# A two-layer mLSTM and retention trunk: order of the state product, one score split on VectorE, later rotary tables, and a last row tile in two column groups

## The chip, the cores and the metric

The kernel runs on one core of one Trainium2 chip. The metric is the device time of one execution in microseconds (us); the median of several runs is compared. The profile records one execution with its own time.

## The reference

Two layers of a pre-norm trunk on 1024 tokens of width 1024. Each layer makes one combined projection, feeds four mLSTM heads and four retention heads of 256, gates and normalises each head, multiplies with the output matrix, and adds the result to x. A last RMSNorm follows.

```python
for l in range(DEPTH):
    shift, scale, gate = jnp.split(c_act @ w_ada[l] + b_ada[l], 3, axis=-1)
    h = rmsnorm(x, norm_g[l]) * (1.0 + scale[:, None, :]) + shift[:, None, :]
    mq, mk, mv, mo, mz, mi, mf, rq, rk, rv, rz = split_cols(h @ w_in[l])
    qk = jax.nn.silu(causal_dwconv(jnp.concatenate([mq, mk], axis=-1), conv_w[l], conv_b[l]))
    ...
    y_m = jax.nn.sigmoid(mo) * head_layernorm(cell, gn_m[l], N_HEADS_MLSTM) * jax.nn.silu(mz)
    rq_h = rotary(rq.reshape(B, S, N_HEADS_RET, HD_R), positions)
    rk_h = rotary(rk.reshape(B, S, N_HEADS_RET, HD_R), positions)
    ...
    y_r = head_layernorm(ret, gn_r[l], N_HEADS_RET) * jax.nn.silu(rz)
    y = jnp.concatenate([y_m, y_r], axis=-1) @ w_out[l]
    x = x + gate[:, None, :] * y
return rmsnorm(x, final_g)
```

`rotary` turns the two halves of q and k by angles position x frequency, for the retention heads alone.

## The kernel before, in words

**Products in three matmuls.** Every operand of a product is held as a high part in a short float format and a low part, the rest of it. `mm3` issues high x high, high x low and low x high into one PSUM bank. `split_to(dst, src, eng)` makes the two parts: ScalarE copies (L614), and `eng` subtracts (L615); GpSimd is the default, and the state's split names VectorE.

**Order.** TensorE's order is written by hand. A unit is a piece of TensorE work with what empties its bank; `run_units` calls `tick()` after each. `launch(gen, delay)` puts a generator of side work on a list, and `tick` runs those that are due; the number that a generator yields is the count of steps until its next piece. What comes of this as an order of calls decides TensorE's instructions. The other engines' orders follow from these calls through a scheduler that places each instruction on its engine; once built, every engine runs strictly in its order, and waits at an instruction whose data or buffer isn't ready.

**A layer.** Per head group hg (0 to 3 mLSTM, 4 to 7 retention): `gate_path` (z and o columns), `qk_ml` or `qk_ret` (q, then k), and `v_path`. They write four PSUM banks `pp` in turn. For mLSTM, `conv_silu` reads a bank with VectorE products (L632), takes three columns over from the half before (L634), goes through a tanh on ScalarE (L636) and a product (L637). For k the result is also transposed (L644) and stored to DRAM; `k_rows` reads it back. `v_split` reads a bank with ScalarE (L600) and VectorE (L601).

**Attention** runs as side work beside the projections of the next group, on four banks `pa`. Four pieces of 256 tokens, j = 0 to 3; those in `WHOLE` are taken as one, the others as two tiles of 128. `scores(j)` multiplies q and k, applies the mask `dm` (from a transfer, L748 and L750, and an exponential) with VectorE (L780 or L789, then L790), and splits the result into `sH` and `sL`. `update` adds to the running state `cf` (L818) and splits it into `cH` and `cL` on VectorE. `values(j, tts)` multiplies q with the state parts (j > 0; L839 takes it to `nd`), then the scores with v, and L851 adds the two.

**Rotary tables.** `rotary_tables` makes, in four pieces of 256 positions, the reduced angles for sine and cosine. Each piece is one load of positions (L374), 26 VectorE instructions on three 512-wide tiles taken from the pool `g` (six tiles, shared with the gates of L543 and L553), and two stores to the DRAM tensors `rdr` (L403). `a1`, half of one of those tiles, is written by a copy early in each piece (L378) and is the source of the cosine's store. `load_rotary` reads `rdr` back when head group 3's attention ends. The launch stands at the end of head group 1's turn in layer 0.

**The end.** `out_units` multiplies with the output matrix. For the last half and column block (`done` given) twelve of the sixteen k pieces go over four row tiles together, into four banks; the last four go row tile by row tile. After each, `out_evac` multiplies by the gate (L997), adds x (L998), and sums squares (L1001). `final_rows` then makes the row's scale with a power on GpSimd (L1036, L1037); `final_scale` applies it to the two column blocks with ScalarE and VectorE (L1028, L1030) and stores (L1031).

Of the kernel before, what the change touches and what calls it, by code (L numbers as in the profile page):

```python
# [19 lines left out]
P = 128  # L20
# [60 lines left out]
def tile_hybrid_trunk(ctx, tc, x, c, positions, w_ada, b_ada, norm_g, w_in, conv_w, conv_b,  # L81
# [38 lines left out]
    def launch(gen, delay=0):  # L120
        uid[0] += 1
        pending.append([clock[0] + delay, uid[0], gen])
# [490 lines left out]
    def split_to(dst, src, eng=G):  # L613
        A.copy(dst[0], src)  # L614
        eng.tensor_tensor(dst[1], src, f(dst[0]), ALU.subtract)  # L615
# [120 lines left out]
    def attention(l, hg, gt, qT, kT, kt, vs, gp, rot):  # L736
# [30 lines left out]
        def scores(j):  # L767
            half, jo = j // 2, (j % 2) * CH
            dmat = dms.pop(j) if ml else rmask
            ps = ps_a()  # L770
            sd = wt("th", 512, 5)
            if j in WHOLE:
                pd = ps[:, CH:2 * CH].rearrange("p (a b) -> p a b", a=2)
                for dt in range(2):
                    kk, qq = kT[dt][half], qT[dt][j]
                    ks = slice(jo, jo + P)
                    mm3(ps[:, 0:CH], (kk[0][:, ks], kk[1][:, ks]), (qq[:, 0:CH], qq[:, CH:2 * CH]), dt == 0, dt == 1)
                diagonal(pd, j, 1)
                V.tensor_tensor(sd[:, 0:CH], ps[:, 0:CH], dmat[:, 0:CH], ALU.mult)
                V.tensor_tensor(sd[:, CH:2 * CH].rearrange("p (a b) -> p a b", a=2), pd,  # L780
                                dmat[:, CH:CH + P].unsqueeze(1).to_broadcast([P, 2, P]), ALU.mult)
                V.tensor_tensor(sd[:, CH:CH + P], sd[:, CH:CH + P], sd[:, CH + P:2 * CH], ALU.add)
                n = CH + P
            else:
                p4, s4 = (x.rearrange("p (t a b) -> p t a b", t=2, a=2) for x in (ps, sd))
                for tt in range(2):
                    diagonal(p4[:, tt], j, tt)
                m = dmat[:, 0:CH].rearrange("p (t b) -> p t b", t=2) if ml else dmat[:, CH:CH + P].unsqueeze(1)
                V.tensor_tensor(s4, p4, m.unsqueeze(2).to_broadcast([P, 2, 2, P]), ALU.mult)  # L789
                V.tensor_tensor(s4[:, :, 0], s4[:, :, 0], s4[:, :, 1], ALU.add)  # L790
                n = CH
            s2 = (wt("sH", 384, 2, F32R)[:, 0:n], wt("sL", 384, 2, F32R)[:, 0:n])
            if j in WHOLE:
                split_to(s2, sd[:, 0:n])
            else:
                split_to([x.rearrange("p (t b) -> p t b", t=2) for x in s2], s4[:, :, 0])
            sds[j] = s2
            dm_load(j + 2)
# [23 lines left out]
        def values(j, tts):  # L822
            state = st["state"]
            sH, sL = sds[j]
            if tts[0] == 0:
                st["nd"] = wt("nd", 516, 1).rearrange("p (a b) -> p a b", a=2) if ml else None
                nrm[j] = wt("n", 512, 1).rearrange("p (a b) -> p a b", a=2)
            nd3 = st["nd"]
            src = {}
            for tt in tts:  # L830
                pi = None
                if j > 0:
                    pi = ps_a()
                    for dt in range(2):
                        qq = qT[dt][j]
                        mm3(pi[:, 0:W], (qq[:, tt * P:(tt + 1) * P], qq[:, CH + tt * P:CH + (tt + 1) * P]),
                            (state[0][:, dt, 0:W], state[1][:, dt, 0:W]), dt == 0, ml and dt == 1)
                    if ml:
                        A.activation(nd3[:, tt, 0:W], pi[:, 0:W], AF.Copy,  # L839
                                     scale=gt["wi"][:, h, 2 * j + tt - 2:2 * j + tt - 1])  # L840
                acc = not ml and j > 0
                po = pi if acc else ps_a()
                sources = [(tt, tt * P)]
                if j in WHOLE:
                    sources = [(si, 256 if si else tt * P) for si in range(tt + 1)]
                for n, (si, so) in enumerate(sources):
                    mm3(po[:, 0:W], (sH[:, so:so + P], sL[:, so:so + P]),
                        (vs[j][0][:, si, 0:W], vs[j][1][:, si, 0:W]), n == 0 and not acc, n == len(sources) - 1)
                if ml:
                    if j > 0:  # L850
                        V.tensor_tensor(nd3[:, tt, 0:W], po[:, 0:W], nd3[:, tt, 0:W], ALU.add)  # L851
                    else:
                        A.copy(nd3[:, tt, 0:W], po[:, 0:W])
                else:
                    src[tt] = po[:, 0:HD]
            if not ml:
                normalise(j, tts, src)
            elif tts[-1] == 1:
                normalise(j, (0, 1), [nd3[:, tt, 0:HD] for tt in range(2)])
# [105 lines left out]
    def out_units(l, half, cc, loads, gb, xnew, ss, done=None):  # L965
        banks = [ps_a() if cc else ps_p() for _ in range(4)]

        def product(k, piece, tt):
            (yH, yL), w = piece
            ts = slice(tt * P, (tt + 1) * P)  # L970
            mm3(banks[tt], (yH[:, ts], yL[:, ts]), w, k == 0, k == 15)

        together = 12 if done else 16
        for k in range(together):
            piece = loads.take()
            for tt in range(4):
                product(k, piece, tt)
            yield
        if not done:
            out_evac(l, half, cc, banks, gb, xnew, ss, range(4))  # L980
        else:
            pieces = [loads.take() for _ in range(together, 16)]
            for tt in range(4):
                for k in range(together, 16):
                    product(k, pieces[k - together], tt)
                out_evac(l, half, cc, banks, gb, xnew, ss, (tt,))
                done((tt,))
                yield

    def out_evac(l, half, cc, banks, gb, xnew, ss, rows):  # L990
        for tt in rows:
            row = half * 4 + tt
            xr = bt()
            srcx = x[row * P:(row + 1) * P] if l == 0 else xdr[row]
            Q.dma_start(xr, srcx[:, cc * 512:(cc + 1) * 512])
            tmp = wt("th", 512, 5)
            V.tensor_tensor(tmp, banks[tt], gb[cc], ALU.mult)  # L997
            V.tensor_tensor(xr, xr, tmp, ALU.add)  # L998
            if l < DEPTH - 1:
                Q.dma_start(xdr[row][:, cc * 512:(cc + 1) * 512], xr)  # L1000
            A.activation(tmp, xr, AF.Square, accum_out=ss[:, tt, cc:cc + 1])  # L1001
            xnew[tt][cc] = xr

    def new_ss():
        return cst.tile([P, 8], F32, tag="ss", bufs=2, name=nm("ss")).rearrange("p (a b) -> p a b", a=4)
# [98 lines left out]
    for l in range(DEPTH):  # L1104
# [103 lines left out]
        for hg in range(8):  # L1208
            ml = hg < 4
            if hg == 0:  # L1210
                rot = [[], []]
            if hg > 0:
                gp = gp1 if hg == 1 else [[None, None], [None, None]]
                run_units(gate_path(l, hg, hT, gp, 0, 1 if hg == 7 else 2, hg > 1 or l > 0))
            vs = []
            kt = [None] * NCH
            kT = [[None, None], [None, None]]
            qT = [[None] * NCH, [None] * NCH]
            if hg == 4:
                run_units(v_path(l, hg, hT, gt, vs))  # L1220
            for which, res in ((0, qT), (1, kT)):
                if ml:
                    run_units(qk_ml(l, hg, which, hT, gt, kt, res))
                else:
                    run_units(qk_ret(l, hg % 4, which, hT, kt, res, *rot))
            if 0 < hg < 4:
                launch(attention(l, hg, gt, qT, kT, kt, vs, gp, rot), 4 if hg == 3 else 7)
            if hg not in (0, 4):
                run_units(v_path(l, hg, hT, gt, vs))
            if hg == 0:  # L1230
                launch(v0_splits(gt, vraw, vs), 1)
            if hg == 0 or hg > 3:
                launch(attention(l, hg, gt, qT, kT, kt, vs, gp, rot), 2 if hg == 0 else 0)
            if hg == 7:
                loads = OutLoads(l)
                for _ in gate_path(l, hg, hT, gp, 1):
                    loads.stage()
                    tick()
            if hg == 1 and l == 0:
                launch(rotary_tables(), 0)  # L1240
            if hg == 5:
                launch(gate_rows(l, gb))
            if hg == 3 and l + 1 < DEPTH:
                launch(ada_columns_later(l + 1))
# [52 lines left out]
```

## Time and profile before

| | |
|---|---|
| median of 3 runs | 2310.84 us (2310.66 to 2312.41) |
| the profiled execution | 2311.88 us |
| its span | 2310.0 us |
| TensorE instructions | 12447 matmuls, as many weight loads |
| transfers | 259.44 MB, mean 112 GB/s |
| granted TensorE clock, mean | 0.997 of full speed |

Busy time counts an instruction from start to end. Matmuls are pipelined, so a 512-wide matmul is shown with 0.39 us while the next starts 0.23 us after it; the distance of starts tells what one costs. DVE is VectorE, ACT ScalarE, POOL GpSimd, SP SyncE, which issues the transfers. In a timeline row the columns are start, duration, engine, line, operation, tiles and shape, then in brackets the idle time before it and what ended it. In a row of windows each engine's busy time is followed by its count of instructions. `L615` is line 615 of the kernel before.

### The profile page before, as it was taken

The numbers are of one execution on the slowest core, as the hardware profiler recorded it, in microseconds if no ns is written. First come the engines' busy times: TensorE is split into PE (matmuls) and PEld (weight loads), VectorE is DVE, ScalarE is ACT, GpSimd is POOL, SyncE is SP. The second block draws the span as 40 slices with busy tenths as digits, with TensorE's granted clock in tenths as the row PEclk, the third lists the DMA queues.
The fourth block names the chain that finished last, engine by engine and source line by source line (L and its number), as shares of the span: only waits on it lengthen the run. The fifth ranks groups of instructions, "written<-read, shape, count | busy, mean of one in ns | idle before, by whom it ended". The sixth has DMA issues, their size and how long they took to land.

```text
span 2310.0 us, 34281 instructions
## 1 busy us (share of the span) xinstructions
PE 2277.8 (99%) x12447; PEld 1958.2 (85%) x12447; DVE 1353.2 (59%) x2835; ACT 907.1 (39%) x1768; POOL 823.5 (36%) x817
## 2 busy tenths in 40 slices
PE   7999999999999999999999999999999999999998
PEld 5888888889988888888888889888898888988886
DVE  7477688556555555584536665555563545556753
ACT  5535433444332323353434544344443323224442
POOL 1343424333343334222552434233334334341323
PEclk9999999999999999999999999999999999999999
DMA  8223232324433533486532322322323333436762
GB/s 257 80 64 98 73 84 80 82 74 116 120 109 88 150 83 87 128 258 217 177 92 57 84 72 77 84 74 69 81 70 89 81 87 93 124 81 205 240 231 78
DMA packets 328761, 259.44 MB, mean 112 GB/s; under 512 B 79732, under 2 KB 263804, under 8 KB 328592
## 3 DMA queue, kind: packets, MB, share of 16 engines
q1 hardware_dynamic: 328592, 257.27, 38.6%
q8 instruction: 97, 1.59, 0.3%
q14 instruction: 72, 0.59, 0.1%
HBM read 201.58 MB, written 55.61 MB: 111 GB/s over the span
## 4 chain that ended last, share of the span: by engine, by line
PE 91%; DVE 3%; DMA 3%; issue 1%; POOL 1%; ACT 1%; SPq 0%; POOLq 0%; DVEq 0%; ACTq 0%
PE pp L145 24%; PE pp L146 24%; PE pp L147 24%; PE pa L146 5%; PE pa L147 5%; PE pa L145 5%; PE pa L765 2%; DMA b<-in_w_ada_dram 1%; DMA b<-in_x_dram 1%; PE pa L315 0%; DMA raw<-in_w_ada_dram 0%; POOL wL L615 0%; POOL sL L615 0%; DVE b L266 0%; DMA b<-in_w_in_dram 0%
## 5 line engine op out<-in xcount | busy, mean ns | idle before, releaser
L145 PE MATMUL pp<-b,wH 128*128 128x512 f32 x1776 | 703.7, 396 | 1.1 <-ACT b L1137 1.1
L146 PE MATMUL pp<-b,wH 128*128 128x512 f32 x1776 | 700.2, 394 | 0.3 <-DVE b L1140 0.2
L147 PE MATMUL pp<-b,wL 128*128 128x512 f32 x1776 | 700.2, 394 | 0.0
L615 POOL TENSOR_TENSOR wL<-raw,wH 128x512 fp32r<-128x512 f32 x338 | 450.1, 1338 | 507.4 <-ACT wH L614 466.8
L147 PEld LDWEIGHTS pp<-b,wL 128*128 128x128 f32 x1776 | 333.9, 188 | 79.0
L146 PEld LDWEIGHTS pp<-b,wH 128*128 128x128 f32 x1776 | 334.2, 188 | 72.2 <-DVE b L1140 2.0
L145 PEld LDWEIGHTS pp<-b,wH 128*128 128x128 f32 x1776 | 334.4, 188 | 71.5 <-ACT b L1137 1.6
L614 ACT CAST wH<-raw 128x512 fp32r<-128x512 f32 x402 | 246.1, 616 | 322.8 <-PE pp L147 93.8
L145 PE MATMUL pp<-wH,b 128*128 128x256 f32 (+1 forms) x1152 | 353.0, 306 | 0.7 <-DVE g L543 0.7
L147 PE MATMUL pp<-wH,b 128*128 128x256 f32 (+1 forms) x1152 | 352.8, 306 | 0.0
L146 PE MATMUL pp<-wL,b 128*128 128x256 f32 (+1 forms) x1152 | 352.2, 306 | 0.0
L615 POOL TENSOR_TENSOR b<-acc,b 128x256 fp32r<-128x256 f32 (+1 forms) x208 | 200.8, 984 | 322.8 <-ACT b L614 315.2
L145 PEld LDWEIGHTS pp<-wH,b 128*128 128x128 f32 x1152 | 216.9, 188 | 12.3 <-DVE g L543 1.6
L147 PEld LDWEIGHTS pp<-wH,b 128*128 128x128 f32 x1152 | 216.6, 188 | 11.4
L146 PEld LDWEIGHTS pp<-wL,b 128*128 128x128 f32 x1152 | 216.7, 188 | 10.8
L632 DVE SCALAR_TENSOR_TENSOR acc<-pp,cols,acc 128x511 f32<-128x511 f32 (+2 forms) x192 | 142.5, 742 | 43.2 <-ACT acc L627 41.2
L614 ACT CAST b<-acc 128x256 fp32r<-128x256 f32 (+1 forms) x208 | 93.7, 487 | 187.4 <-DVE acc L709 127.6
L615 POOL TENSOR_TENSOR sL<-th,sH 128x384 fp32r<-128x384 f32 (+1 forms) x64 | 61.0, 953 | 236.5 <-ACT sH L614 171.9
L145 PE MATMUL pa<-wH,b 128*128 128x512 f32 x256 | 101.1, 395 | 0.0
L147 PE MATMUL pa<-wH,b 128*128 128x512 f32 x256 | 101.0, 394 | 0.0
L146 PE MATMUL pa<-wL,b 128*128 128x512 f32 x256 | 100.9, 394 | 0.0
L636 ACT ACTIVATE th<-acc 128x512 f32<-128x512 f32 x64 | 40.5, 632 | 146.3 <-DVE acc L634 79.3
(255 smaller groups left out, 3439.3 us busy)
## 6 DMA issues: line engine op xcount, KB each, us to landing
raw<-in_w_in_dram SPq DMA_DIRECT2D x274, 256.0 KB
raw<-in_w_out_dram SPq DMA_DIRECT2D x128, 256.0 KB
gdr<-g SPq DMA_DIRECT2D x64, 256.0 KB
ndr<-zt SPq DMA_DIRECT2D x128, 128.0 KB
raw<-in_w_ada_dram SPq DMA_DIRECT2D x64, 256.0 KB
g<-gdr SPq DMA_DIRECT2D x64, 256.0 KB
acc<-ndr SPq DMA_DIRECT2D x64, 256.0 KB
acc<-kdr SPq DMA_DIRECT2D x192, 64.0 KB
```

Of the source, the lines that this page charges most:

```text
L145: PE.matmul(o, lt[0], rt[0], start=start, stop=False)
L146: PE.matmul(o, lt[0], rt[1], start=False, stop=False)
L147: PE.matmul(o, lt[1], rt[0], start=False, stop=stop)
L614: A.copy(dst[0], src)
L615: eng.tensor_tensor(dst[1], src, f(dst[0]), ALU.subtract)
L632: V.scalar_tensor_tensor(acc[:, d:], pt[:, 0:HALF - d], wcol, acc[:, d:], ALU.mult, ALU.add)
L636: A.activation(th, acc, AF.Tanh, scale=0.5)
L765: PE.matmul(pd, kk[i][:, o:o + P], qd, start=dt == 0 and i == 0, stop=dt == 1 and i == 1)
```

## The change

Four edits.

1. In `values`, the six matmuls on the state go over the parts first: high x high and low x high for both dt, and then high x low for both. Before, each dt had its three in a row.
2. In `scores`, the low part of head group 0's first scores (j = 0, both layers) is subtracted on VectorE; before, on GpSimd as all others.
3. `rotary_tables` is launched with a delay of 14 steps instead of 0.
4. In the last half and column block, row tile 3 is multiplied in two groups of 256 columns, the second into a bank of its own from the other pool. The last four k pieces run for the first group and then for the second. A new `last_evac` empties the two groups one after the other, sums their squares apart, and adds these.

```diff
             if j in WHOLE:
-                split_to(s2, sd[:, 0:n])
+                split_to(s2, sd[:, 0:n], V if hg + j == 0 else G)
...
                     pi = ps_a()
-                    for dt in range(2):
-                        qq = qT[dt][j]
-                        mm3(pi[:, 0:W], (qq[:, tt * P:(tt + 1) * P], qq[:, CH + tt * P:CH + (tt + 1) * P]),
-                            (state[0][:, dt, 0:W], state[1][:, dt, 0:W]), dt == 0, ml and dt == 1)
+                    for part in range(2):
+                        for dt in range(2):
+                            qq = qT[dt][j]
+                            for i in range(2 - part):
+                                PE.matmul(pi[:, 0:W], qq[:, i * CH + tt * P:i * CH + (tt + 1) * P],
+                                          state[part][:, dt, 0:W], start=part + dt + i == 0,
+                                          stop=ml and part + dt == 2)
...
+        if done:
+            tail = ps_p()
+
-        def product(k, piece, tt):
+        def product(k, piece, tt, parts=(0, 1)):
             (yH, yL), w = piece
             ts = slice(tt * P, (tt + 1) * P)
-            mm3(banks[tt], (yH[:, ts], yL[:, ts]), w, k == 0, k == 15)
+            if done and tt == 3:
+                for i in parts:
+                    o = tail[:, 0:256] if i else banks[3][:, 0:256]
+                    mm3(o, (yH[:, ts], yL[:, ts]), [x[:, i * 256:(i + 1) * 256] for x in w], k == 0, k == 15)
+            else:
+                mm3(banks[tt], (yH[:, ts], yL[:, ts]), w, k == 0, k == 15)
...
             for tt in range(4):
-                for k in range(together, 16):
-                    product(k, pieces[k - together], tt)
-                out_evac(l, half, cc, banks, gb, xnew, ss, (tt,))
+                for parts in ((0,), (1,)) if tt == 3 else ((0, 1),):
+                    for k in range(together, 16):
+                        product(k, pieces[k - together], tt, parts)
+                if tt == 3:
+                    last_evac(half, cc, (banks[3], tail), gb, xnew, ss)
+                else:
+                    out_evac(l, half, cc, banks, gb, xnew, ss, (tt,))
                 done((tt,))
...
+    def last_evac(half, cc, parts, gb, xnew, ss):
+        row = half * 4 + 3
+        xr = bt()
+        Q.dma_start(xr, xdr[row][:, cc * 512:(cc + 1) * 512])
+        tmp = wt("th", 512, 5)
+        s2 = wt("sm1", 4, 2)
+        for i in range(2):
+            cs = slice(i * 256, (i + 1) * 256)
+            V.tensor_tensor(tmp[:, cs], parts[i][:, 0:256], gb[cc][:, cs], ALU.mult)
+            V.tensor_tensor(xr[:, cs], xr[:, cs], tmp[:, cs], ALU.add)
+            A.activation(tmp[:, cs], xr[:, cs], AF.Square, accum_out=s2[:, i:i + 1])
+        V.tensor_tensor(ss[:, 3, cc:cc + 1], s2[:, 0:1], s2[:, 1:2], ALU.add)
+        xnew[3][cc] = xr
...
             if hg == 1 and l == 0:
-                launch(rotary_tables(), 0)
+                launch(rotary_tables(), 14)
```

## The prediction

> **What bounds the kernel now.** The page first: the engines, and the chain that ended last.
>
> ```profile
> PE 2277.8 (99%) x12447; PEld 1958.2 (85%) x12447; DVE 1353.2 (59%) x2835; ACT 907.1 (39%) x1768; POOL 823.5 (36%) x817
> PE 91%; DVE 3%; DMA 3%; issue 1%; POOL 1%; ACT 1%; SPq 0%; POOLq 0%; DVEq 0%; ACTq 0%
> ```
>
> TensorE runs in an order written by hand and is almost never idle, so the change is worth what it takes from or adds to TensorE's waits, and to the tail after its last matmul. Next, TensorE's waits stretch by stretch. Three rows are 315 to 339 us, the attention of head group 1 in layer 0; the last is of the whole span. Behind the colon stand the sum, the count and the longest.
>
> ```profile
> PE pa L145 <- DVE th L780: 1.0, 1, 1.0
> PE pa L145 <- ACT nd L839: 0.7, 1, 0.7
> PE pa L146 <- DVE cL L615: 0.7, 2, 0.4
> ...
> PE pa L146 <- DVE cL L615: 1.7, 4, 0.5
> ```
>
> They are idle time after the modelled end of a matmul, and that undercounts, as one wait in the timeline shows:
>
> ```profile
> 924.42 0.28 PE L145 MATMUL pa<-cH,b 128*128 128x256 f32 x1
> 925.23 0.39 PE L146 MATMUL pa<-cL,b 128*128 128x256 f32 x1 [0.53 <-DVE cL L615]
> 925.46 0.28 PE L147 MATMUL pa<-cH,b 128*128 128x256 f32 x1
> ```
>
> A 256-wide matmul "lasts" 0.28, but the next one starts 0.12 after it where nothing is late (the two-group part below works from the same distance). So a wait shown as 0.53 costs 925.23-924.42-0.12 = 0.69, that is 0.16 more, and 0.1 again since the start behind it comes 0.23 later and not 0.12. The four waits of head group 1 cost 2.4+4x0.26 = 3.4 us; a shorter one not listed brings it to about 3.6. That is what rotary work costs today: VectorE has it between the scores (L780) and the state's low part (L615), and SyncE issues the mask load of the next scores (L748) only behind the positions load (L374):
>
> ```profile
> 308.82 0.34 SPq L374 DMA_DIRECT2D g<-in_positions_dram  x1
> 309.42 0.34 SPq L748 DMA_DIRECT2D dm<-mdr  x1
> ```
>
> **The rotary tables, 14 steps later.** First the gain. In the changed order the tables' first instruction stands where head group 1's attention ends (about 338 us of this trace); the 3.6 us go.
>
> Then what they meet. VectorE's tables are 104 instructions. Busy time of all instructions on g tiles (the tables' scratch) in two windows, then of all of VectorE:
>
> ```profile
> 294.00:388.00 94.00, 48.82 (x111) 1.00 0.30 78
> 338.00:401.40 63.40, 23.61 (x53) 1.00 0.28 76
> 338.00:401.40 63.40, 53.00 (x127) 1.00 0.28 76
> ```
>
> Of the 111 seven are gates (L543, L553; about 0.68 each), which leaves 44.1 us for 104, mean 0.424. Of the 53, three are gates: 21.5 us of tables, so 31.5 us of other work. The changed order has 73 table instructions ahead of the transposition at 400.66 below: 73x0.424 = 31.0, and 31.0+31.5 = 62.5 us of work in 63.4. Today 10.4 us of that window are idle, mostly VectorE waiting for ScalarE inside a convolution; table instructions between fill some of it, not all. If none of the idle time had to stay, VectorE would arrive on time; if all, 9.5 us late. I take 3.
>
> Behind that transposition the changed order puts 25 more table instructions in a row, ahead of the convolution that empties a PSUM bank. The rows today: the transposition, the convolution's first and last product from the bank, and the matmul of the v path that writes the bank next (four banks in rotation); then the last read of the following bank, and its next matmul.
>
> ```profile
> 400.66 0.71 DVE L644 STREAM_TRANSPOSE th<-acc 128x512 f32<-128x512 f32 x1
> 402.51 0.75 DVE L632 SCALAR_TENSOR_TENSOR acc<-pp,cols,acc 128x511 f32<-128x511 f32 x1 [1.14 <-ACT acc L627]
> 404.64 0.73 DVE L632 SCALAR_TENSOR_TENSOR acc<-pp,cols,acc 128x509 f32<-128x509 f32 x1
> ...
> 411.77 0.28 PE L145 MATMUL pp<-wH,b 128*128 128x256 f32 x1
> ...
> 412.49 0.48 DVE L601 SCALAR_TENSOR_TENSOR b<-pp,eul,b 128x256 fp32r<-128x256 f32 x1 [0.47 <-ACT b L600]
> ...
> 417.43 0.40 PE L145 MATMUL pp<-b,wH 128*128 128x512 f32 x1
> ```
>
> The bank is free at 405.37 and wanted at 411.77: slack 6.4 us. The 25 instructions are 14 with one tensor operand and 11 with two. Rows of single ones, a copy into a1 (L378), and one caught beside GpSimd:
>
> ```profile
> 315.37 0.29 DVE L400 TENSOR_SCALAR g<-g 128x256 f32<-128x256 f32 x1
> 317.44 0.26 DVE L378 CAST g<-g 128x256 fp32r<-128x256 f32 x1
> 318.28 1.29 POOL L615 TENSOR_TENSOR wL<-raw,wH 128x512 fp32r<-128x512 f32 x1 [1.48 <-ACT wH L614]
> 318.33 1.52 DVE L380 TENSOR_TENSOR g<-g,g 128x256 f32<-128x256 f32 x1
> 329.22 0.42 DVE L391 TENSOR_TENSOR g<-g,g 128x256 f32<-128x256 f32 x1
> ```
>
> Undisturbed they take 14x0.29+11x0.42 = 8.7 us, at the mean 25x0.424 = 10.6. Among them L378 writes a1, which the table before still stores to DRAM (L403): from L400 to L378 passed 2.07 us above. So 10.8 to 12.7 us stand where 1.14 us of waiting stood, and the bank comes free 9.7 to 11.5 us later; less the slack, 3.3 to 5.1 us of TensorE stall, of which I take 4, since GpSimd is less busy there than around 318. With 3 us of lateness the new wait, of a v-path matmul for L632's bank, is 7 us; bounds 3.3 and 5.1+9.5 = 14.6.
>
> Its follow-up. While VectorE is late, the next bank's last read (412.97, 7.6 us behind the first bank's) is late too, by up to six more table instructions (2.1 us), and TensorE wants that bank 417.43-411.77 = 5.7 us after restarting: a second wait of 7.6-5.7 = 1.9 to 4 us. But a long stall also changes the clock. At the start TensorE, busy 1.4 of 3.5 us, fell to half clock; PEclk stands behind the busy time, and 512-wide matmuls start 0.43 apart instead of 0.23:
>
> ```profile
> 24.00:27.40 3.40, 2.99 (x6) 2.11 (x7) 3.37 (x8) 3.30 (x10) 0.00 (x0) 0.50 1.09 365
> 27.40:30.80 3.40, 3.40 (x11) 2.65 (x10) 2.85 (x10) 0.67 (x3) 1.19 (x1) 0.59 1.10 350
> ...
> 26.15 0.63 PE L145 MATMUL pp<-b,wH 128*128 128x512 f32 x1
> 26.58 0.63 PE L146 MATMUL pp<-b,wH 128*128 128x512 f32 x1
> ```
>
> That cost 3.4x0.50+3.4x0.41 = 3.1 us. After a stall of 7 us I expect the same, and a slower TensorE then reaches the second bank when it is free. So the two do not add: together 2.9, bounds 0 (short stall, VectorE catches up) and 4. The Trainium skill, "TensorE: Matmul & The Clock Gate", Part 1: The HAM clock gate, says that an idle window of about 3.4 us halves the clock and that one busy window of that length restores it. The trace agrees on the half, but its slow stretch was longer; by the page's figure the term would be an estimated 1.7 and the sum 1.2 us lower.
>
> Rotary: -3.6+7+2.9 = +6.3.
>
> **State's low part last.** In each of a row tile's six matmuls on the state, cL is now first read by the fifth and not the second: 3x0.12 = 0.36 us of slack. Two of the four cL waits of the whole span lie outside head group 1 (0.5 shown, about 0.69 real); each loses 0.36 and keeps the rest. Shorter ones under the view's sight add a little: -1.0, bounds -0.7 and -1.5. Instructions and weight loads stay the same in number.
>
> **Head 0's first low scores on VectorE.** GpSimd's instruction and VectorE's neighbours, layer 0 and then layer 1, with TensorE's wait in layer 1:
>
> ```profile
> 188.35 1.01 POOL L615 TENSOR_TENSOR sL<-th,sH 128x384 fp32r<-128x384 f32 x1 [5.16 <-ACT sH L614]
> 188.85 0.80 DVE L790 TENSOR_TENSOR th<-th 128x256 f32<-128x256 f32 x1
> ...
> 1314.93 1.76 POOL L615 TENSOR_TENSOR sL<-th,sH 128x384 fp32r<-128x384 f32 x1 [4.49 <-ACT sH L614]
> 1315.42 0.41 DVE L790 TENSOR_TENSOR th<-th 128x256 f32<-128x256 f32 x1
> ...
> PE pa L147 <- POOL sL L615: 0.9, 1, 0.9
> ```
>
> No row has 128x384 on VectorE; between 0.41 for 256 and 0.75 for 511 I estimate 0.55. It takes the place of L790. Layer 1: done at 1315.97 instead of 1316.69, -0.7. Layer 0: 189.40 instead of 189.36, nothing; but GpSimd, now free, goes straight to a weight split (L615, 1.29), and where that starts first VectorE stands behind it as L380 did above: 0 to +1.3, I take half, +0.6. The Trainium skill, "SBUF — State Buffer", SBUF: two separate sides, calls this an exclusive lock taken by whichever starts first; 318.28 and 318.33 agree, and by it alone the layer 0 term would be 0 or 1.3, never half.
>
> **Last row tile in two column groups.** 48 matmuls of 512 columns become 96 of 256; the tail today:
>
> ```profile
> 2300.72 0.39 PE L146 MATMUL pa<-wL,b 128*128 128x512 f32 x1
> 2300.95 0.40 PE L147 MATMUL pa<-wH,b 128*128 128x512 f32 x1
> ...
> 2302.28 0.92 POOL L1037 TENSOR_TENSOR nrmr<-nrm,mhalf 128x1 f32<-128x1 f32 x1 [2.48 <-DVE nrm L1036]
> 2303.24 0.75 DVE L1028 SCALAR_TENSOR_TENSOR b<-b,nrmr,b 128x512 f32<-128x512 f32 x1 [0.43 <-POOL nrmr L1037]
> ...
> 2304.61 0.21 DVE L1036 TENSOR_SCALAR nrm<-ss 128x1 f32<-128x1 f32 x1 [0.61 <-ACT th L1001]
> 2305.48 0.75 DVE L1028 SCALAR_TENSOR_TENSOR b<-b,nrmr,b 128x512 f32<-128x512 f32 x1 [0.66 <-POOL nrmr L1037]
> ```
>
> TensorE: 0.23 becomes 2x0.118, +0.2. The second group's product then takes some 0.4 instead of 0.69, but in VectorE's new order its addition stands behind row tile 2's scaling, which waits for GpSimd's power (2302.28): with 0.55 for that power when it is not held up (0.92 was), scaling runs 2302.9 to 2303.6, addition to 2304.0, square and its read 0.6, one more addition of sums 0.2, then nrm at about 2304.8 against 2304.61. Together +0.3, bounds -0.7 (the halves' time saved) and +0.8.
>
> **Sum.** +6.3-1.0-0.7+0.6+0.3 = +5.5. The profiled run took 2311.88, 1.04 over the median of the runs; on the median, 2310.84+5.5 = 2316.3 us.
>
> **The rivals.**
> - A, VectorE keeps up and the slack covers the rest, no new wait: -3.6-1.4+0.3 to +0.6, about -4.9, 2306. For it: 6.4 us of slack, and waits inside convolutions that table work can fill. Against: 25 instructions in a row need more than the slack, even undisturbed. Decides at a bank delay of 6.4.
> - B, a stall of 3 to 4 without lateness before it, too short for the clock: -3.6+3.5-0.8 = -0.9, 2310. For it: 62.5 of 63.4 us does just fit.
> - C, all idle time of the window stays: stall 12, clock and second bank 4: -3.6+16-0.8 = +11.6, 2322. For it: the collisions with GpSimd in the mean may recur in a fuller window.
> - D, the move does not free head group 1, because its waits come from attention itself: +5.5+3.6 = +9.1, 2320. Against: L374 stands ahead of L748 in the rows.
>
> **How the numbers follow.** My forecast 43%, A 22%, B 20%, C 9%, D 6%. The range reaches from A's time to near C: 2306.5 to 2321.5; the forecast's own is 2312 to 2321. 0.2% (4.6 us, about what a measurement of this kernel tells from no change) puts the borders at 2306.2 and 2315.5. Slower: three quarters of the forecast, C and D, 0.48. Faster: most of A, 0.18. Same: the rest, 0.34.
>
> **What would show it.** Right: no TensorE wait between 310 and 340; one wait of several us of a v-path matmul (pp L145) for L632 near 408, PEclk at 0.5 behind it, L378 waiting for a transfer just before; no cL wait above 0.2; layer 1's sL wait under 0.3. Wrong: no wait of pp on L632, or waits in head group 2's attention instead; a last scaling before 2305 less what TensorE gained would contradict the tail.

## The result, and the profile after

The changed kernel takes 2314.49 us (median of 22 runs, 2313.51 to 2316.0), the kernel before 2311.55 beside it (22 runs, 2310.29 to 2312.76): ratio 1.0014, 95% interval 1.0007 to 1.0020. It is slower by some 3 us, where +5.5 was forecast. The profiled execution has a span of 2312.9 us against 2310.0.

TensorE's waits in the changed kernel, over the whole span first (sum, count, longest):

```profile
PE pp L145 <- DVE acc L634: 6.2, 1, 6.2
...
PE pa L147 <- DVE sL L615: 0.8, 2, 0.6
...
PE pa L147 <- POOL sL L615: 0.4, 1, 0.4
...
PE pa L838 <- DVE cL L615: 0.2, 1, 0.2
```

The three rows of head group 1 are gone; between 300 and 340 us there is no wait at all. In their place stands one of 6.2 us, on a PSUM bank `pp` that VectorE empties (the view names L634, the small instruction right behind L632). cL is down to a single listed wait of 0.2. Of the two waits for sL on VectorE, 0.6 is layer 0's, as before, and 0.2 layer 1's, where it was 0.9.

VectorE ahead of that wait, with the first matmuls behind it:

```profile
399.04 0.70 DVE L644 STREAM_TRANSPOSE th<-acc 128x512 f32<-128x512 f32 x1
399.67 0.76 DVE L397 TENSOR_SCALAR g<-g 128x256 f32<-128x256 f32 x1
400.47 1.41 DVE L398 TENSOR_TENSOR g<-g,g 128x256 f32<-128x256 f32 x1
...
403.23 0.29 DVE L400 TENSOR_SCALAR g<-g 128x256 f32<-128x256 f32 x1
405.36 0.29 DVE L378 CAST g<-g 128x256 fp32r<-128x256 f32 x1 [1.83 <-DMA rdr<-g]
...
411.58 0.74 DVE L632 SCALAR_TENSOR_TENSOR acc<-pp,cols,acc 128x511 f32<-128x511 f32 x1
...
413.15 0.74 DVE L632 SCALAR_TENSOR_TENSOR acc<-pp,cols,acc 128x509 f32<-128x509 f32 x1
...
414.04 0.55 PE L145 MATMUL pp<-wH,b 128*128 128x256 f32 x1 [6.15 <-DVE acc L634]
414.39 0.41 PE L146 MATMUL pp<-wL,b 128*128 128x256 f32 x1
414.60 0.41 PE L147 MATMUL pp<-wH,b 128*128 128x256 f32 x1
```

From the transposition's end (399.74) to the convolution (411.58) pass 11.8 us; before it was 1.1. Twenty-five table instructions fill them, with 1.83 us of waiting for a store in the middle. Behind the wait matmuls of 256 columns start 0.21 apart instead of 0.12. The windows there (TensorE busy, granted clock, share and GB/s of the transfers) show why:

```profile
410.30:414.00 3.70, 0.00 (x0) 0.50 0.00 0
414.00:417.10 3.10, 3.06 (x14) 0.50 0.06 19
417.10:420.00 2.90, 2.90 (x27) 1.00 0.41 130
```

The clock fell to half during the wait, at 410.3 us, and was whole again at 417.1, some 3 us after the wait's end.

Where the time went, by the start of the same matmul in both traces:

| at | before | after | later by |
|---|---|---|---|
| first product of layer 0 | 24.41 | 24.81 | 0.40 |
| behind head 0's first cL wait | 228.30 | 228.39 | 0.09 |
| behind head group 1's attention | 338.29 | 334.29 | -4.00 |
| the bank wait | 411.77 | 414.04 | 2.27 |
| the next bank of the v path | 417.43 | 421.18 | 3.75 |
| behind head group 2's first sL | 428.28 | 432.71 | 4.43 |
| retention in layer 0 | 926.30 | 929.98 | 3.68 |
| behind layer 1's first sL | 1316.98 | 1319.97 | 2.99 |
| behind layer 1's last cL wait | 2056.52 | 2059.03 | 2.51 |
| last matmul | 2300.95 | 2303.82 | 2.86 |

The 0.40 at the top arises ahead of everything the change touches.

### The profile page after: what moved, and what is told of

Read it like the earlier page. It is cut to its first block, busy times and chain, and to the rows that moved or that the text cites. A ratio compares the mean times of both kernels' runs of the same rounds, so it can differ in the third digit from the quotient of the medians.

```text
span 2312.9 us, 34379 instructions
## 1 busy us (share of the span) xinstructions
PE 2275.8 (98%) x12495; PEld 1961.1 (85%) x12495; DVE 1350.6 (58%) x2840; ACT 905.9 (39%) x1770; POOL 818.8 (35%) x815
## 4 chain that ended last, share of the span: by engine, by line
PE 54%; DVE 1%; POOL 1%; issue 0%; ACT 0%; DMA 0%; POOLq 0%; DVEq 0%; ACTq 0%
PE pp L145 14%; PE pp L146 14%; PE pp L147 14%; PE pa L147 3%; PE pa L145 3%; PE pa L146 3%; PE pa L838 2%; PE pa L765 1%; POOL b L615 0%; PE pa L315 0%; DMA raw<-in_w_in_dram 0%; DVE b L1057 0%; DVE b L1013 0%; DVE b L310 0%; DVE th L1012 0%
## 5 line engine op out<-in xcount | busy, mean ns | idle before, releaser
L145 PE MATMUL pp<-wH,b 128*128 128x256 f32 (+1 forms) x1168 | 358.5, 307 | 6.8 <-DVE acc L634 6.2
L146 PE MATMUL pp<-wL,b 128*128 128x256 f32 (+1 forms) x1168 | 357.8, 306 | 0.0
L147 PE MATMUL pp<-wH,b 128*128 128x256 f32 (+1 forms) x1168 | 357.6, 306 | 0.0
L145 PEld LDWEIGHTS pp<-wH,b 128*128 128x128 f32 x1168 | 220.5, 189 | 18.6 <-issue 6.3
L147 PEld LDWEIGHTS pp<-wH,b 128*128 128x128 f32 x1168 | 220.3, 189 | 11.5
L632 DVE SCALAR_TENSOR_TENSOR acc<-pp,cols,acc 128x511 f32<-128x511 f32 (+2 forms) x192 | 142.5, 742 | 39.4 <-ACT acc L627 37.5
L615 POOL TENSOR_TENSOR sL<-th,sH 128x256 fp32r<-128x256 f32 (+1 forms) x62 | 58.1, 936 | 212.7 <-ACT sH L614 149.0
L145 PE MATMUL pa<-wH,b 128*128 128x512 f32 (+1 forms) x256 | 99.2, 388 | 0.0
L147 PE MATMUL pa<-wH,b 128*128 128x512 f32 (+1 forms) x256 | 99.2, 387 | 0.0
L146 PE MATMUL pa<-wL,b 128*128 128x512 f32 (+1 forms) x256 | 99.0, 387 | 0.0
```

Source lines behind the costliest of these rows:

```text
L145: PE.matmul(o, lt[0], rt[0], start=start, stop=False)
L146: PE.matmul(o, lt[0], rt[1], start=False, stop=False)
L147: PE.matmul(o, lt[1], rt[0], start=False, stop=stop)
L632: V.scalar_tensor_tensor(acc[:, d:], pt[:, 0:HALF - d], wcol, acc[:, d:], ALU.mult, ALU.add)
```

## The experiments

Each run was timed beside the kernel before on the same chip, whose median there was 2312.57 us in the first four and 2312.1 in the others; the ratios count.

**The later tables alone**, on the kernel before:

```diff
-                launch(rotary_tables(), 0)
+                launch(rotary_tables(), 14)
```

> The kernel before with the later rotary tables alone. Theory (the later tables are the whole loss: head group 1's waits gone, 4.1 us in the trace; new bank wait 6.3; half clock 1.5; a late sL in head group 2, 0.6): +4.3 us on before, about 2315.8, so slower than the full change by about 1.3. Rival (the tables as such gain, and the other three edits lose): below before by about 3.6, 2308.

Measured: 2317.15 us, ratio 1.0021 (1.0012 to 1.0029). Its waits from 300 to 480 us are the same two as in the full change:

```profile
PE pp L145 <- DVE acc L634: 6.2, 1, 6.2
PE pa L147 <- POOL sL L615: 0.4, 1, 0.4
```

So the move of the tables by itself loses at least what the full change loses: 4.6 us against 2.9 by the medians, with intervals that overlap. That the other three edits gain is what this difference suggests; the next run asks for it.

**The other three edits**, with the tables where they were:

```diff
-                launch(rotary_tables(), 14)
+                launch(rotary_tables(), 0)
```

> The full change with the tables launched at 0 again. Theory: cL waits shorter by 0.36 each (six of them, -2.0), layer 1's sL wait 0.7 shorter, tail +0.3: -2.4 us on before, about 2309.1. Rival (the other edits lose what the full change loses): 2314 or more.

Measured: 2311.41, ratio 0.9994 (0.9985 to 1.0003); the sign as expected, the gain half as large, and the interval takes in no change, so the times alone do not show a gain. In the trace the last matmul starts 2.1 us earlier than before, but in this execution the end came 0.7 later behind it. Head group 1 kept most of its waits:

```profile
PE pa L145 <- DVE th L780: 1.0, 1, 1.0
PE pa L145 <- ACT nd L842: 0.5, 1, 0.5
PE pa L838 <- ACT cH L614: 0.4, 1, 0.4
```

The third row is new: with cL needed later, one tile there now waits for cH instead. So the low part used last was worth less in that stretch than 0.36 a tile.

**The cosine into another scratch**, to take the transfer out of the run of 25:

```diff
-            parts = ((1, 0.0, tmp), (0, 0.25, a1))
+            parts = ((1, 0.0, tmp), (0, 0.25, rnd))
```

> The full change, but the cosine angles are written to the scratch rnd instead of a1, so that the next table's copy into a1 does not wait for their transfer to DRAM. Theory: L378's wait of 1.83 us in the run of 25 is gone and the bank wait falls from 6.3 to about 4.4; with the half clock still there 2312.6, without it 2311.1. Rival (VectorE's backlog alone sets the convolution, the transfer is hidden anyway): bank wait 6.3, 2314.5.

Measured: 2317.46, ratio 1.0020 (1.0011 to 1.0029); above the full change's 1.0014, though the intervals overlap, where both theories had it better or equal. VectorE between the transposition and the convolution:

```profile
400.99 0.70 DVE L644 STREAM_TRANSPOSE th<-acc 128x512 f32<-128x512 f32 x1
...
406.49 0.29 DVE L388 TENSOR_SCALAR g<-g 128x256 f32<-128x256 f32 x1 [1.79 <-DMA rdr<-g]
...
412.99 0.29 DVE L400 TENSOR_SCALAR g<-g 128x256 f32<-128x256 f32 x1
413.20 0.74 DVE L632 SCALAR_TENSOR_TENSOR acc<-pp,cols,acc 128x511 f32<-128x511 f32 x1
```

The wait did not go, it moved a few instructions on: the next table's first write to `rnd` (L388) comes too soon behind the store. And with other dependences the schedule put the tables' last six instructions ahead of the convolution too. The run from the transposition to the convolution is about as long as in the full change (11.5 us against 11.8), but it begins 2 us later. The bank wait was 8.3 us. The edit didn't test what it was meant to, so the share that the store's 1.83 us has in the loss stays open; what it does show is that with more table work ahead of L632 in all, the wait is longer.

**Launched 20 steps later:**

```diff
-                launch(rotary_tables(), 14)
+                launch(rotary_tables(), 20)
```

> The full change with the tables launched 20 steps later instead of 14. In its order 12 table instructions instead of 25 stand in a row ahead of the convolution, and 18 come later, among head group 2's first evacuations of v. Theory (the row of table instructions ahead of the convolution sets the stall): 13 fewer at 0.36 take 4.7 us off, bank wait under 2, no half clock, about 2308.5. Rival (the work only moves its wait, to the next bank or the scores): a wait of 3 or more at the banks behind, 2312 or more.

Measured: 2313.98, ratio 1.0006 (0.9997 to 1.0015). Both were right, at different places. TensorE's waits from 400 to 440 us, VectorE's rows there, and GpSimd's beside the last four:

```profile
PE pp L145 <- DVE b L601: 5.9, 2, 5.2
...
405.20 0.74 DVE L632 SCALAR_TENSOR_TENSOR acc<-pp,cols,acc 128x511 f32<-128x511 f32 x1
...
414.29 1.39 DVE L387 TENSOR_SCALAR g<-g 128x256 f32<-128x256 f32 x1
415.60 1.51 DVE L383 SCALAR_TENSOR_TENSOR g<-g 128x256 f32<-128x256 f32 x1
417.04 1.38 DVE L388 TENSOR_SCALAR g<-g 128x256 f32<-128x256 f32 x1
418.34 1.51 DVE L384 SCALAR_TENSOR_TENSOR g<-g 128x256 f32<-128x256 f32 x1
...
414.19 5.37 POOL L615 TENSOR_TENSOR wL<-raw,wH 128x512 fp32r<-128x512 f32 x4 [3.08 <-DMA acc<-kdr]
```

The wait for L632 is gone. But the fourth table now stands ahead of the evacuation of v (L601), each of these four instructions held up to 1.4 or 1.5 us beside GpSimd's splits, and the same kind of wait appears one bank further on, 5.2 us long, with the half clock behind it.

**Launched at the start**, where VectorE was 17% busy:

```diff
         vraw = []
+        if l == 0:
+            launch(rotary_tables(), 0)
...
-            if hg == 1 and l == 0:
-                launch(rotary_tables(), 14)
```

> The full change, but the tables are launched in layer 0 ahead of head 0's v and gate projections (before, 75 to 105 us: VectorE busy 5.2 of 30 us, TensorE without a wait from 55 to 135) instead of behind head group 1. Theory (the tables cost only where they stand ahead of an evacuation that a PSUM bank's next user soon needs): no bank wait at 414, no half clock, none of head group 1's waits, about 6 us below before, 2306. Rival (table work costs wherever it stands, as waits for it move along): new waits of several us between 75 and 200, of pp on L439 or of head group 0's attention on the gate chain, 2310 or more.

Measured: 2323.48, ratio 1.0049 (1.0032 to 1.0066). The theory fell here. TensorE's waits from 80 to 110, 140 to 160 and 185 to 210 us:

```profile
PE pa L446 <- DVE g L440: 6.3, 3, 2.9
...
PE pa L506 <- DVE b L496: 2.6, 1, 2.6
...
PE pa L145 <- ACT sH L614: 2.2, 1, 2.2
```

The banks were not what mattered there: the transposes of the gates (L446) need the small copies that stood behind tables, and the gate chain on VectorE (L496) ran late into the next transposes (L506). The third wait was not followed to its cause.

**The same at once**, with all instructions issued at that place:

```diff
-            launch(rotary_tables(), 0)
+            for _ in rotary_tables():
+                pass
```

> As the early launch, but all table instructions are issued at that place at once instead of over 68 steps, so that they end earlier and stand a few at a time inside the gate chain. Theory: the same 2306; if the gate chain's lateness costs something in the early launch, this one differs by that. Rival: it delays the small copies from the banks (L439), a wait of pp above 1 us between 75 and 110, 2308 or more.

Measured: 2324.39, ratio 1.0052 (1.0037 to 1.0067). The rival's loss held, but not by the wait that it named: none of `pp` is listed there. The transposes' waits for L440 were 6.9 us together, and that for L496 5.5.

**The end in another order.** Row tile 2's scaling, in the order by hand, stands behind row tile 3's last addition and square:

```diff
-                    last_evac(half, cc, (banks[3], tail), gb, xnew, ss)
+                    with tc.manual_schedule():
+                        last_evac(half, cc, (banks[3], tail), gb, xnew, ss, done)
+                        done((3,))
...
             A.activation(tmp[:, cs], xr[:, cs], AF.Square, accum_out=s2[:, i:i + 1])
+            done((2,), 1 + i)
```

Here `done((2,), 1)` makes row tile 2's power, `done((2,), 2)` its scaling.

> The full change with the end in an order by hand: row tile 2's scaling stands behind row tile 3's second addition on VectorE and behind its square on ScalarE. Theory (the two column groups gain nothing only because that addition waits behind the scaling, 0.7 us, and its power): from the last matmul's start to the last scaling 4.53 us in the full change as before, here about 3.6; total 0.9 below the full change, 2314. Rival (the chain is set by the extra sum and the powers): 4.4 or more, no difference.

Measured: 2314.35, ratio 1.0009 (1.0000 to 1.0018), the full change having 1.0014. In the full change, and then here:

```profile
2303.82 0.28 PE L147 MATMUL pp<-wH,b 128*128 128x256 f32 x1
...
2305.56 0.75 DVE L1057 SCALAR_TENSOR_TENSOR b<-b,nrmr,b 128x512 f32<-128x512 f32 x1 [0.32 <-POOL nrmr L1066]
2306.23 0.42 DVE L1028 TENSOR_TENSOR b<-b,th 128x256 f32<-128x256 f32 x1
...
2308.35 0.75 DVE L1057 SCALAR_TENSOR_TENSOR b<-b,nrmr,b 128x512 f32<-128x512 f32 x1 [0.72 <-POOL nrmr L1066]
```

```profile
2304.43 0.28 PE L147 MATMUL pp<-wH,b 128*128 128x256 f32 x1
...
2305.90 0.43 DVE L1031 TENSOR_TENSOR b<-b,th 128x256 f32<-128x256 f32 x1
2306.24 0.75 DVE L1061 SCALAR_TENSOR_TENSOR b<-b,nrmr,b 128x512 f32<-128x512 f32 x1
...
2308.03 0.75 DVE L1061 SCALAR_TENSOR_TENSOR b<-b,nrmr,b 128x512 f32<-128x512 f32 x1 [0.72 <-POOL nrmr L1073]
```

From the last matmul to the last scaling 4.53 us became 3.60, as expected: the addition no longer stands behind the scaling. By the medians the total is 2.2 us above the kernel before, against 2.9 for the full change; that fits, but the two intervals overlap. The profiled executions differ by 0.3 only, since the half clock cost more in this one (see the last section).

**The fourth table apart**, with three tables as in the full change (`rotary_tables` takes the pieces to make as an argument here):

```diff
-                launch(rotary_tables(), 14)
+                launch(rotary_tables(range(3)), 14)
+                launch(rotary_tables(range(3, 4)), 56)
```

> The full change, but only three of the four tables are launched at 14; the fourth has tiles of its own and is launched at 56. In its order 7 table instructions instead of 25 stand ahead of the convolution, and the fourth table stands in ones to fours among head group 2's last attention pieces. Theory (the run ahead of the convolution is the whole loss): 18 fewer at 0.33 and no transfer wait take 7.8 us off a lateness that exceeded the slack by 6.3, so no bank wait, no half clock: full change less 6.3, 1.5 and what the late sL cost, 0.5; before less 5.5 to 6, ratio 0.9975. Rival (the fourth table's work moves the wait, as with 20 steps): a new wait of 2 us or more between 420 and 560, ratio 0.9985 or more.

Measured: 2307.13, ratio 0.9979 (0.9970 to 0.9988), faster than the kernel before and than the full change. TensorE's only wait listed from 300 to 600 us, and VectorE's step from the third table to the convolution:

```profile
PE pa L147 <- POOL sL L615: 0.5, 1, 0.5
...
403.06 0.29 DVE L400 TENSOR_SCALAR g<-g 128x256 f32<-128x256 f32 x1
403.27 0.74 DVE L632 SCALAR_TENSOR_TENSOR acc<-pp,cols,acc 128x511 f32<-128x511 f32 x1
```

Up to 403 us VectorE runs as in the full change; without the 18 instructions and the transfer the convolution starts 8.3 us earlier, and there is neither a wait nor a half clock. The late sL stayed, though nothing was late: that part of the expectation was wrong.

**Both together**, the fourth table apart and the end's order by hand (the two diffs above):

> As the later fourth table, with the end in the order by hand as well. If the two are independent: 0.9 us less, before less about 6.7, ratio 0.9971; last matmul's start to last scaling 3.6 again.

Measured: 2306.29, ratio 0.9975 (0.9965 to 0.9984), the lowest of all, with an interval that overlaps the one above. The last scaling starts 3.6 us behind the last matmul again. That matmul starts at 2296.26 in its trace and the span ends at 2304.6; 8.3 us apart, against 9.3 without the order by hand (2296.59 and 2305.9).

## Why the prediction was right, and where it was off

- **Bank wait behind the tables.** The mechanism, its place and its size held: 7 forecast, 6.3 measured. The later tables alone bring exactly this wait, and taking 18 instructions away, with the wait for the store among them, removes it. Its two terms hold too. VectorE's lateness was taken as 3 us; the transposition started at 399.04 where 400.66 less TensorE's lead of 4.0 would be on time, so 2.4. The run was to delay the convolution by 9.7 to 11.5; it was 11.84-1.14 = 10.7. Less the slack, 2.4+10.7-6.4 = 6.7; the convolution itself then emptied the bank in 2.31 us instead of 2.86.
- **Head group 1 freed.** 3.6 forecast, 4.1 in the table. Rival D, that these waits are attention's own, falls.
- **Rival A and B** fall with the wait itself. Six point four us of slack did not cover 25 instructions. (A's terms as written add up to -4.7 to -4.4, not to -4.9.) **Rival C** falls as well; VectorE filled most of the idle time.
- **Second bank or half clock.** Here lies the largest part of the miss: 2.9 taken, 1.5 measured (2.27 to 3.75 in the table). The step that failed is the reading that the clock would cost what it had cost at the start, 3.1 us, as if that were a fixed price. The half clock lasted as long here (410.3 to 417.1) as at the start of the kernel before (23.4 to 30.2), 6.8 us; but here 3.7 of them lay inside the wait, where TensorE had nothing to do, and only 3.1 behind it. How the half clock falls to the wait is not the same in each execution: in the run with the end by hand the same wait of 6.15 us was followed by 5.7 us at half clock, and from the restart to the next bank's first matmul TensorE took 8.31 us, where it took 7.14 in the full change and 5.66 before. There the clock cost 2.65, near the 2.9 forecast; with the tables alone it cost 1.6. So that the term came out as low as 1.5 is in part the luck of one execution. The second bank was not waited for, as argued: at half clock TensorE came late enough. The Trainium skill, "TensorE: Matmul & The Clock Gate", Part 1: The HAM clock gate, has one busy window of about 3.4 us bring the clock back. By it the term was an estimated 1.7: nearer to the 1.5 of the full change than the row that was preferred, and farther from the 2.65 of the run by hand.
- **cL.** 1.0 forecast; the table shows 0.31 less at 228, 0.75 between 432 and 930 (two cL waits, near 572 and 926) and 0.48 before 2059: about 1.5, the upper bound.
- **Head 0's sL.** Layer 1: 0.7 forecast, 0.7 measured (3.68 to 2.99 in the table). Layer 0: half of a lost race was taken (+0.6), but VectorE came first and nothing was lost. GpSimd's split stood behind it and took 1.96 us:

```profile
189.27 0.55 DVE L615 TENSOR_TENSOR sL<-th,sH 128x384 fp32r<-128x384 f32 x1
...
189.35 1.96 POOL L615 TENSOR_TENSOR wL<-raw,wH 128x512 fp32r<-128x512 f32 x1 [5.73 <-DMA acc<-kdr]
```

  The estimate of 0.55 us for 128x384 was exact. Taking the middle of a race that can only be won or lost was the wrong choice.
- **The end.** +0.3 forecast and +0.3 measured, but all of it on TensorE: from the last matmul to the last scaling 4.53 us passed in both traces. The order by hand shows the reason given, the addition behind the scaling.
- **What the sum lacked.** A late sL in head group 2, 0.7 us (3.75 to 4.43 in the table). In the changed order ScalarE takes the next mask's exponentials (L757) ahead of the copy sH:

```profile
430.14 0.70 ACT L757 ACTIVATE dm<-dm,COL 128x128 f32<-128x128 f32 x2 [0.95 <-POOL dm L756]
430.74 0.50 ACT L614 CAST sH<-th 128x384 fp32r<-128x384 f32 x1
```

  It is in every run with the tables at 14 whose waits are shown here, the one without a bank wait too, so it belongs to the order, not to the lateness. That the exponentials ahead of sH are its cause was not tried by itself.

Sum of the measured terms: -4.1+6.3+1.5+0.7-1.5-0.7+0.3 = +2.5, and the 0.4 at the start makes the 2.9 between the two spans. The 0.4 is of these two executions; that the medians hold it too is not shown. Forecast and result differ by 2.6. What came out lower than forecast adds up to 3.7: the clock 1.4, the bank wait 0.7, the race 0.6, head group 1 and cL 0.5 each. The late sL and the start give 1.1 of it back.

## What to carry to other kernels

Work without a due time is not free on an engine that is 59% busy: it costs where an in-order engine has it ahead of something that TensorE needs soon. So look in the order for the longest run of it and price that run against the slack of the buffer behind it, and not against the engine's idle share: the launch at the start went where VectorE was 17% busy, and lost 11 us. Where one piece too many stands in the wrong place, move that piece and leave the others: with three of the four tables at the new place the change gained 5 us, with all four it lost 3.

## What the runs showed of the hardware that was not expected

Six of the kernels have a wait of TensorE of 5.2 to 8.3 us: the full change, the tables alone, the other scratch, 20 steps later, the early tables at once, and the end by hand. In each of the six its clock fell to half during the wait, and stayed there for 3.0 to 5.7 us behind it. The length of the wait does not set this: in the run with the end by hand, where TensorE restarted at 413.67 us after the same 6.15 us as in the full change, the half clock lasted until 419.4. In the rows of windows the clock is the number behind the busy time:

```profile
412.60:416.00 3.40, 2.33 (x11) 0.50 0.00 0
416.00:419.40 3.40, 3.40 (x18) 0.50 0.38 122
```

In the first of these rows TensorE was busy for 2.33 of 3.40 us and stayed at half clock for the next 3.4; in the full change it was whole again after 3.1.

Nor does it take one long wait. In the early launch a wait of 2.6 us left the clock whole (the first two rows). Two groups of short waits halved it, with matmuls between them: 1.0, 2.9 and 2.4 us between 98 and 106, and 2.2 and 0.6 us between 202 and 206.

```profile
149.90:153.00 3.10, 0.57 (x5) 1.00 0.00 1
153.00:156.40 3.40, 3.29 (x17) 1.00 0.90 81
...
99.90:103.30 3.40, 0.36 (x2) 1.00 0.09 27
103.30:106.70 3.40, 1.11 (x4) 0.51 0.15 50
...
202.30:205.70 3.40, 0.82 (x4) 1.00 0.75 214
205.70:209.10 3.40, 3.40 (x13) 0.51 0.47 92
```

So no length of a single wait parts the two cases. What does part them was not tried.
